# Rotary embedding on one core: the first two slabs in halves through the engines, and the last slab stored in two halves

## Chip, cores and metric

The kernel runs on one core of a Trainium2 chip. The time is device time in microseconds (us), the median over several executions. Kernels that are compared ran on the same chip in the same rounds. A ratio is the mean time of one kernel's fast runs over the mean of the other's fast runs of the same rounds, so it isn't quite the ratio of the medians that are quoted beside it. A difference counts as faster or slower from 2%.

## The reference

```python
batch, seq, dim, num_heads = 16, 512, 1024, 16      # x: float32
x = x.reshape(batch, seq, num_heads, head_dim)       # head_dim 64
x1, x2 = x[..., :32], x[..., 32:]
rotated = np.concatenate([x1 * cos - x2 * sin,
                          x1 * sin + x2 * cos], axis=-1).astype(np.float32)
```

The input and the output are 33.55 MB each, and there are a few operations per element. The cosine and sine tables are 64 KB each.

## The kernel before

The data goes through in 8 slabs of two batches, each [128 x 8192] float32, 4 MB. There are five buffers ("slots"). SyncE issues the loads, ACT issues the stores, so loads and stores have a DMA queue each. Per slab, ACT casts float32 to bfloat16, DVE makes two multiplications and an addition, and ACT casts the result back into the slab, from where it is stored. Load s+5 can only be issued when store s has landed.

```python
    nb = 2; slots = 5
    ...
    load(0)
    ... # the two tables, issued from GpSimd
    for s in range(1, slots):          # loads 1 to 4 wait for the first table
        tc.add_manual_dep(load(s).ins, table[0].ins.name, ...)
    ...
    passes = []
    for s in range(nslabs):
        n = rpp if s < nslabs - 2 else rpp // 2      # the last two slabs in halves
        passes += [(s, r, n) for r in range(0, rpp, n)]

    cast(passes[0])
    for i, (s, r, n) in enumerate(passes):
        if i + 1 < len(passes):
            cast(passes[i + 1])
        ...
        for t, a in ((t2, rpp * hd), (xu, 0)):
            nc.vector.tensor_mul(out=t, in0=xu, in1=view(tab, ...))
        nc.vector.tensor_add(out=xu, in0=xu, in1=view(t2, ...))
        nc.scalar.copy(out=xs, in_=xu)
        if r + n == rpp:
            nc.scalar.dma_start(out=dram(out_flat, s), in_=slab[s])
            if s + slots < nslabs:
                load(s + slots)
```

Of the kernel before, what the change touches and what calls it, by code (L numbers as in the profile page):

```python
# [2 lines left out]

# [4 lines left out]


@with_exitstack  # L10
def kernel(
    ctx: ExitStack,
    tc: tile.TileContext,
    x: bass.AP,
    cos: bass.AP,
    sin: bass.AP,
    num_heads: int,
    out: bass.AP,
):
    nc = tc.nc  # L20
    P = nc.NUM_PARTITIONS

    batch, seq, dim = x.shape
    nh = num_heads
    hd = dim // nh
    half = hd // 2
    bf16 = mybir.dt.bfloat16
    f32 = mybir.dt.float32

    nb = 2  # L30
    slots = 5
    nslabs = batch // nb
    rpp = nb * seq // P
    W = rpp * dim
    SP = seq // rpp
    TW = rpp * half

    out_flat = out.rearrange("b s h d -> b s (h d)")

    singles = ctx.enter_context(tc.tile_pool(name="singles", bufs=1))  # L40
    slabs = ctx.enter_context(tc.tile_pool(name="slabs", bufs=slots))
    xpool = ctx.enter_context(tc.tile_pool(name="xpool", bufs=2))
    psum = ctx.enter_context(tc.tile_pool(
        name="psum", bufs=1, space=bass.MemoryType.PSUM))


    def dram(t, s, a=0, n=W):
        return bass.AP(tensor=t.tensor, offset=t.offset + s * nb * seq * dim + a,
                       ap=[[W, P], [1, n]])


    def view(t, offset, *dims):
        return dataclasses.replace(t, offset=t.offset + offset,
                                   ap=[t.ap[0], *[list(d) for d in dims]])


    slab = {}


    def load(s):  # L60
        slab[s] = slabs.tile([P, W], f32, tag="slab", name="slab")
        return nc.sync.dma_start(out=slab[s], in_=dram(x, s))  # L62


    load(0)


    TR = seq // P
    G = rpp // TR
    table = {}  # L70
    raw = singles.tile([P, 2 * TR * half], f32, tag="raw")
    for i, src in enumerate((cos, sin)):
        table[i] = nc.gpsimd.dma_start(out=view(raw, i * TR * half, (1, TR * half)), in_=bass.AP(  # L73
            tensor=src.tensor, offset=src.offset,
            ap=[[TR * half, P], [1, TR * half]]))



    for s in range(1, slots):
        tc.add_manual_dep(  # L80
            load(s).ins, table[0].ins.name,
            mybir.DependencyInfo(mybir.DependencyClass.Sync,
                                 mybir.DependencyReason.DATA),
            reason="issue")


    pick = singles.tile([P, G * P], bf16, tag="pick")
    nc.gpsimd.memset(pick, 0.0)  # L88
    for g in range(G):
        part = view(pick, g * P, (SP, P // SP), (1, SP))  # L90
        nc.gpsimd.affine_select(  # L91
            out=part, in_=part, compare_op=mybir.AluOpType.not_equal, fill=1.0,
            base=-g, pattern=[[0, P // SP], [-G, SP]], channel_multiplier=1)

    tab1 = singles.tile([P, 2 * TR * half], bf16, tag="tab1")
    nc.vector.tensor_copy(out=tab1, in_=raw)  # L96
    acc = psum.tile([P, 2 * TW], f32, tag="acc")
    for i in range(2):
        for g in range(G):
            nc.tensor.matmul(view(acc, i * TW + g * TR * half, (1, TR * half)),  # L100
                             view(pick, g * P, (1, P)),
                             view(tab1, i * TR * half, (1, TR * half)),
                             start=True, stop=True)

    tab = singles.tile([P, 2 * rpp * hd], bf16, tag="tab")
    nc.vector.tensor_copy(out=view(tab, 0, (hd, 2 * rpp), (1, half)),  # L106
                          in_=view(acc, 0, (half, 2 * rpp), (1, half)))
    nc.vector.tensor_copy(out=view(tab, half, (hd, rpp), (1, half)),  # L108
                          in_=view(acc, 0, (half, rpp), (1, half)))
    nc.vector.tensor_scalar_mul(  # L110
        out=view(tab, rpp * hd + half, (hd, rpp), (1, half)),
        in0=view(acc, TW, (half, rpp), (1, half)), scalar1=-1.0)

    xb = {}


    def cast(u):
        s, r, n = u
        if r == 0:
            xb[s] = xpool.tile([P, W], bf16, tag="xb", name="xb")  # L120
        nc.scalar.copy(out=view(xb[s], r * dim, (1, n * dim)),  # L121
                       in_=view(slab[s], r * dim, (1, n * dim)))



    passes = []
    for s in range(nslabs):
        n = rpp if s < nslabs - 2 else rpp // 2
        passes += [(s, r, n) for r in range(0, rpp, n)]


# [4 lines that stand above are left out]
        xs = view(slab[s], r * dim, (1, n * dim))  # L136
        xu = view(xb[s], r * dim, (1, n * dim))

        t2 = view(slab[s].bitcast(bf16), 2 * r * dim, (1, n * dim))
        for t, a in ((t2, rpp * hd), (xu, 0)):  # L140
            nc.vector.tensor_mul(  # L141
                out=t, in0=xu,
                in1=view(tab, a + r * hd, (hd, n), (0, nh), (1, hd)))
        nc.vector.tensor_add(  # L144
            out=xu, in0=xu, in1=view(t2, half, (hd, n * nh), (-half, 2), (1, half)))

        nc.scalar.copy(out=xs, in_=xu)  # L147
        if r + n == rpp:
            nc.scalar.dma_start(out=dram(out_flat, s), in_=slab[s])  # L149
            if s + slots < nslabs:  # L150
                load(s + slots)


# [1 line left out]
_INS = ['x', 'cos', 'sin', 'num_heads']  # L155
_OUTS = [((16, 512, 16, 64), 'float32')]

_NUMBERS = {'num_heads': 16}


# [26 lines left out]
```

## Time and profile before

| what | before |
|---|---|
| time, median (range) | 162.97 us (162.37 to 163.03, 3 runs) |
| span of the profiled run | 160.1 us |
| DVE, ACT busy | 108.7 us, 113.5 us |
| DMA: loads + stores + tables, share of 16 engines | 98.1% |
| moved | 67.24 MB |

The profiled execution of the kernel before took 161.85 us, a little less than the three timed ones.

The prediction below shows most of the lines. Two more are needed here. The first is the summary of the chain of work that ended last, from the page of the kernel before. The second is the first store in its timeline (start in us, duration in us, engine's queue, line).

```profile
DMA 43%; ACT 34%; DVE 13%; issue 1%; ACTq 0%; SPq 0%
```
```profile
41.06 0.38 ACTq L149 DMA_DIRECT2D out_dram<-slab  x1
```

### The profile page before, as it was taken

The numbers are of one execution on the slowest core, as the hardware profiler recorded it, in microseconds if no ns is written. First come the engines' busy times: TensorE is split into PE (matmuls) and PEld (weight loads), VectorE is DVE, ScalarE is ACT, GpSimd is POOL, SyncE is SP. The second block draws the span as 40 slices with busy tenths as digits, with TensorE's granted clock in tenths as the row PEclk, the third lists the DMA queues.
The fourth block names the chain that finished last, engine by engine and source line by source line (L and its number), as shares of the span: only waits on it lengthen the run. The fifth ranks groups of instructions, "written<-read, shape, count | busy, mean of one in ns | idle before, by whom it ended". The sixth has DMA issues, their size and how long they took to land.

```text
span 160.1 us, 153 instructions
## 1 busy us (share of the span) xinstructions
PE 0.6 (0%) x4; PEld 0.4 (0%) x4; DVE 108.7 (68%) x34; ACT 113.5 (71%) x21; POOL 2.3 (1%) x9
## 2 busy tenths in 40 slices
PE   0010000000000000000000000000000000000000
PEld 0000000000000000000000000000000000000000
DVE  0003089999978997999799659976919779970000
ACT  3006939559899899989993999159998699826000
POOL 5000000000000000000000000000000000000000
DMA  6999999999999999999999999999999999999994
GB/s 221 442 418 393 459 459 393 434 475 401 409 377 475 442 393 434 483 393 401 508 401 393 499 418 393 467 450 393 426 483 401 401 508 401 393 499 418 393 467 188
DMA packets 2368, 67.24 MB, mean 420 GB/s; under 512 B 288, under 2 KB 288, under 8 KB 320
## 3 DMA queue, kind: packets, MB, share of 16 engines
q1 hardware_dynamic: 1152, 33.55, 49.3%
q10 hardware_dynamic: 1152, 33.55, 48.6%
q0 software_dynamic: 64, 0.13, 0.2%
HBM read 33.69 MB, written 33.55 MB: 420 GB/s over the span
## 4 chain that ended last, share of the span: by engine, by line
DMA 43%; ACT 34%; DVE 13%; issue 1%; ACTq 0%; SPq 0%
DMA slab<-in_x_dram 25%; ACT slab L147 18%; DMA out_dram<-slab 17%; ACT xb L121 16%; DVE slab L141 4%; DVE xb L141 4%; DVE xb L144 4%; ACTq L149 0%; ACTq L147 0%; SPq L62 0%
## 5 line engine op out<-in xcount | busy, mean ns | idle before, releaser
L121 ACT CAST xb<-slab 128x8192 bf16<-128x8192 f32 (+1 forms) x10 | 56.5, 5652 | 25.2 <-DMA slab<-in_x_dram 24.0
L147 ACT CAST slab<-xb 128x8192 f32<-128x8192 bf16 (+1 forms) x10 | 56.5, 5650 | 7.2 <-DVE xb L144 7.2
L141 DVE TENSOR_TENSOR slab<-xb,tab 128x8192 bf16<-128x8192 bf16 (+1 forms) x10 | 35.7, 3572 | 21.7 <-ACT xb L121 21.6
L141 DVE TENSOR_TENSOR xb<-xb,tab 128x8192 bf16<-128x8192 bf16 (+1 forms) x10 | 35.7, 3572 | 0.3
L144 DVE TENSOR_TENSOR xb<-xb,slab 128x8192 bf16<-128x8192 bf16 (+1 forms) x10 | 35.7, 3572 | 0.3
L96 DVE CAST tab<-raw 128x256 bf16<-128x256 f32 x1 | 0.3, 294 | 11.2 <-DMA raw<-in_sin_dram 11.2
L121 ACT ACT_TABLE_LOAD x1 | 1.3, 1283 | 0.7 <-PEq L168 0.7
L106 DVE CAST tab<-acc 128x512 bf16<-128x512 f32 x1 | 0.7, 692 | 0.7 <-PE acc L100 0.7
L73 POOL DMA_DIRECT2D raw<-in_cos_dram x1 | 0.7, 674 | 0.8 <-POOLq L168 0.8
L100 PE MATMUL acc<-tab,pick 128*128 128x128 bf16 x4 | 0.6, 300 | 11.5 <-DVE tab L96 11.5
L91 POOL TENSOR_SCALAR_AFFINE_SELECT pick<-pick 128x128 bf16<-128x128 bf16 x2 | 0.5, 288 | 0.1
L73 POOL DMA_DIRECT2D raw<-in_sin_dram x1 | 0.5, 534 | 0.0
L100 PEld LDWEIGHTS <-pick 128*128 128x128 bf16 x4 | 0.4, 126 | 11.4 <-issue 8.2
L110 DVE TENSOR_SCALAR tab<-acc 128x256 bf16<-128x256 f32 x1 | 0.4, 416 | 0.0
L108 DVE CAST tab<-acc 128x256 bf16<-128x256 f32 x1 | 0.4, 415 | 0.0
L88 POOL MEMSET pick<- 128x256 bf16 x1 | 0.3, 330 | 0.0
L168 POOL MEMSET const-float32-0.0<- 128x1 f32 x1 | 0.1, 98 | 0.2 <-issue 0.2
L168 POOL MEMSET const-bfloat16-1.0<- 128x1 bf16 x1 | 0.1, 101 | 0.0
L168 POOL MEMSET const-uint8-127<- 128x1 uint8 x1 | 0.1, 101 | 0.0
L168 POOL MEMSET const-float32-1.0<- 128x1 f32 x1 | 0.1, 99 | 0.0
## 6 DMA issues: line engine op xcount, KB each, us to landing
slab<-in_x_dram SPq DMA_DIRECT2D x8, 4096.0 KB, 26.1
out_dram<-slab ACTq DMA_DIRECT2D x8, 4096.0 KB, 22.9
raw<-in_cos_dram POOLq DMA_DIRECT2D x1, 64.0 KB, 7.2
raw<-in_sin_dram POOLq DMA_DIRECT2D x1, 64.0 KB, 9.2
```

What stands on the lines that cost most here:

```text
L73: table[i] = nc.gpsimd.dma_start(out=view(raw, i * TR * half, (1, TR * half)), in_=bass.AP(tensor=src.tensor, offset=src.offset, ap=[[TR * ...
L88: nc.gpsimd.memset(pick, 0.0)
L91: nc.gpsimd.affine_select(out=part, in_=part, compare_op=mybir.AluOpType.not_equal, fill=1.0, base=-g, pattern=[[0, P // SP], [-G, SP]], c ...
L100: nc.tensor.matmul(view(acc, i * TW + g * TR * half, (1, TR * half)), view(pick, g * P, (1, P)), view(tab1, i * TR * half, (1, TR * half)) ...
L106: nc.vector.tensor_copy(out=view(tab, 0, (hd, 2 * rpp), (1, half)), in_=view(acc, 0, (half, 2 * rpp), (1, half)))
L108: nc.vector.tensor_copy(out=view(tab, half, (hd, rpp), (1, half)), in_=view(acc, 0, (half, rpp), (1, half)))
L110: nc.vector.tensor_scalar_mul(out=view(tab, rpp * hd + half, (hd, rpp), (1, half)), in0=view(acc, TW, (half, rpp), (1, half)), scalar1=-1.0)
L121: nc.scalar.copy(out=view(xb[s], r * dim, (1, n * dim)), in_=view(slab[s], r * dim, (1, n * dim)))
L141: nc.vector.tensor_mul(out=t, in0=xu, in1=view(tab, a + r * hd, (hd, n), (0, nh), (1, hd)))
L144: nc.vector.tensor_add(out=xu, in0=xu, in1=view(t2, half, (hd, n * nh), (-half, 2), (1, half)))
L147: nc.scalar.copy(out=xs, in_=xu)
L168: nc = _bacc.Bacc("TRN2", target_bir_lowering=False, num_devices=1)
```

## The change

The intent is to fill and drain the pipeline faster. In halves, slabs 0 and 1 reach their store sooner. The first half of the last slab can be stored while its second half is still computed, so that only half a store is left after the last write-back. The manual dependency keeps the order of issue and is no semaphore wait.

```diff
-        n = rpp if s < nslabs - 2 else rpp // 2
+        n = rpp if 2 <= s < nslabs - 2 else rpp // 2
@@
-        nc.scalar.copy(out=xs, in_=xu)
-        if r + n == rpp:
+        back = nc.scalar.copy(out=xs, in_=xu)
+        if s == nslabs - 1:
+
+            if r > 0:
+                tc.add_manual_dep(
+                    back.ins, part.ins.name,
+                    mybir.DependencyInfo(mybir.DependencyClass.NoSync,
+                                         mybir.DependencyReason.DATA),
+                    reason="issue")
+            part = nc.scalar.dma_start(
+                out=dram(out_flat, s, r * dim, n * dim), in_=xs)
+        elif r + n == rpp:
             nc.scalar.dma_start(out=dram(out_flat, s), in_=slab[s])
```

## The prediction

> **What bounds the kernel now.** I read the page's engine totals and its DMA queues first, then the waits of the sync queue, then the timeline of the issues. The engine totals and the slices:
>
> ```profile
> PE 0.6 (0%) x4; PEld 0.4 (0%) x4; DVE 108.7 (68%) x34; ACT 113.5 (71%) x21; POOL 2.3 (1%) x9
> ...
> DMA  6999999999999999999999999999999999999994
> ...
> q1 hardware_dynamic: 1152, 33.55, 49.3%
> q10 hardware_dynamic: 1152, 33.55, 48.6%
> q0 software_dynamic: 64, 0.13, 0.2%
> ```
>
> No compute engine is above 71%, but the DMA row is full from the second slice to the last but one. The loads (q1), the stores (q10) and the tables (q0) take 49.3 + 48.6 + 0.2 = 98.1% of 16 engines' span, which is 157.1 of 160.1 us. Only 3.0 us are without a packet. The trace says where those are: the first packet starts at 1.74 us and the last one ends near 158.9, which makes 1.7 + 1.2 = 2.9 us. So there is next to no hole between the first and the last packet. One store takes 0.486 x 160.1 / 8 = 9.7 us of all 16 engines.
>
> The landings agree. The first load has landed at 13.50 us, the last store at 159.20. Between them lie 15 more slab transfers (7 loads, 8 stores): 145.7 / 15 = 9.71 us each, the same while only loads run (13.50, 23.22, 32.94, 42.65), while both directions run, and while only stores run. The mix does not change the rate.
>
> The end of the chain, from the timeline and from the DMA issues of two short windows (the store of slab 6, then that of slab 7; the last number is the time from issue to landing):
>
> ```profile
> 132.50 0.34 ACTq L149 DMA_DIRECT2D out_dram<-slab  x1
> ...
> 146.68 0.34 ACTq L149 DMA_DIRECT2D out_dram<-slab  x1
> ```
> ```profile
> out_dram<-slab ACTq DMA_DIRECT2D x1, 4096.0 KB, 17.0
> ```
> ```profile
> out_dram<-slab ACTq DMA_DIRECT2D x1, 4096.0 KB, 12.5
> ```
>
> The seventh store lands at 132.5 + 17.0 = 149.5 us, the eighth at 146.7 + 12.5 = 159.2. They are 9.7 us apart, one full-rate transfer, so the last store stood behind the one before it for 149.5 - 146.7 = 2.8 us. The **data is ready before the DMA engines are**, even at the very end. The chain of waits names ACT for 34% and DVE for 13%, but it is followed through last releasers and does not show that the queue in front of each store was still full.
>
> **What the Trainium skill says.** "DMA: Bandwidth & Descriptors", Specifications, gives a fabric ceiling of 435 GB/s for the 16 engines. The trace agrees: 4,194,304 bytes in 9.71 us is 432 GB/s, so this kernel is at the ceiling. The same page, Queues, rings and completion order, says that each engine takes turns between its queue rows packet by packet. The trace agrees in the sum: load 4 and store 0 share the engines from about 42.65 and are both in at 62.22 us, two transfers in 19.6 us. "Perfetto Trace Analysis", DMA Optimizations, says that splitting DMAs may let some start sooner if the DMA engines are generally idle; here they are 98% busy, so its condition is not met. "VectorE: DVE Perf Modes", The TRN2 errata, says VectorE and ScalarE pay a fixed cost per instruction. The groups by form agree:
>
> ```profile
> L121 ACT CAST xb<-slab 128x8192 bf16<-128x8192 f32 x6 | 42.1, 7018 | 18.0 <-DMA slab<-in_x_dram 16.7 <-ACT slab L147 1.3
> ...
> L144 DVE TENSOR_TENSOR xb<-xb,slab 128x8192 bf16<-128x8192 bf16 x6 | 26.6, 4425 | 0.2
> ...
> L121 ACT CAST xb<-slab 128x4096 bf16<-128x4096 f32 x4 | 14.4, 3603 | 7.3 <-DMA slab<-in_x_dram 7.3
> ...
> L144 DVE TENSOR_TENSOR xb<-xb,slab 128x4096 bf16<-128x4096 bf16 x4 | 9.2, 2292 | 0.1
> ```
>
> A cast cut in two costs 2 x 3.603 - 7.018 = 0.19 us more, a tensor operation 2 x 2.292 - 4.425 = 0.16 us more.
>
> **The change, part by part.**
>
> Slabs 0 and 1 in halves. This adds 4 casts on ACT (4 x 0.19 = 0.75 us) and 6 operations on DVE (6 x 0.16 = 0.96 us). Both engines wait for loads at that time, so none of it is on the path. What it moves: the first half-cast runs 13.5 to 17.1; DVE works on both halves in the order of the changed program (two multiplies of the first half, one of the second, then its add) and is done with six operations of 2.32 us, pauses included, at 17.1 + 13.9 = 31.0; ACT casts half of slab 1 at 23.2 to 26.8, then writes slab 0 back in halves, the second at 31.0 to 34.6. Store 0 is thus issued at about **34.7 us instead of 41.06**, 6.4 us sooner. Store 1, worked out in the same way, comes at 52.5 instead of 55.45. Store 2 comes at 69.2 instead of 69.80, and there the lead is gone, because ACT and DVE alternate with slab-long steps from then on.
>
> What is that worth? Count transfers. By time t the engines have moved 1 + (t - 13.50) / 9.71 slabs. At 41.06 that is 3.84, while five loads had been issued: 1.16 slabs, or 11 us of work, were still queued. The same sum at each later issue before gives 6.6 us at store 1, between 9 and 20 us at those that follow, 7.2 at store 6 and 2.8 at store 7. It is never zero. Bringing a store forward by 6 us into a queue that already holds 11 us of work changes the order in which the packets go, not when the last one goes. **Worth: 0.0 us.** Loads 3 and 4 now share the engines with store 0 and land later (I estimate 49 and 68 us instead of 42.65 and 59.79), and loads 5 to 7 end within about 3 us of before. I carried this ledger, with even sharing, to the end: stores 6 and 7 would be ready around 134 and 148 us, about 1 us later than before.
>
> The last slab stored in halves. It adds one DMA issue (0.34 us of ACT's sequencer) and turns 128 packets of 32 KiB into 256 of 16 KiB. The trace has packets of 32 KiB at 1.213 us and of 4 KiB (the tables) at 0.159, which is 0.008 us fixed plus 27.2 bytes per ns; eight more packets on each engine are 8 x 0.008 = 0.07 us. What it moves: the first half can be issued after its own write-back, about 141 us, the second about 148. Store 6 keeps the engines busy until 149.5, so the first half stands in line for some 8 us and the second for about 6. **Worth: between 0.0 and 0.1 us lost**, plus the insurance that a last store ready 1 us later than before has no hole in front of it.
>
> The head (1.7 us, and the tables' packets before 13.50) and the tail (0.9 us from the last landing to the end) are untouched. Sum: 162.97 + 0.07, and I round down a little since one of the three runs before was at 162.37: 162.9 us.
>
> **The rivals.** First, the gain that the chain of waits promises: half a store less at the end (9.7 / 2 = 4.9 us) and a pipeline that starts 6.4 us sooner, which would make 158 to 160 us. For it speaks only the chain, and ACT's 24 us of waiting for loads; against it the 2.8 us for which the last store already queued, and the 98%. It needs a hole in the DMA row, and there is none. Second, a new wait: the early stores take engine time from loads 3 and 4, the casts from slab 4 on come later, and the last stores are issued so late that the queue runs dry before them. A delay of 1 us in the middle is covered by the leads; to show, the last slab's first half would have to come over 8 us later. It would make 163.5 to 165 us. Third, costs per packet and per issue of the split store are larger than the tables' packets suggest, or the two directions together cost HBM something at a different overlap: 163.2 to 164. Against it stands that 9.71 us holds in each mix before.
>
> **Range and chances.** With the DMA as bound, the answer is the time before within its scatter; the runs before spread over 0.66 us, and kernels on the same chip agree to about 0.3%, or 0.5 us. I widen that slightly on both sides for the second and third rivals and for a small gain: 162.2 to 163.7. Over 2% is 3.3 us. A gain of that size would need more than all of the 3.0 us without packets; a loss needs a hole that the ledger doesn't show. So 0.02 faster, 0.96 same, 0.02 slower.
>
> **What the profile after would show.** Right, if: the shares of q1 and q10 still add up to about 98% and the DMA row has no slice below 9 inside; store 0 is issued near 34.7 and its landing comes many us after; the last two landings are about 4.9 us apart and the last is at 159 to 159.5; ACT's busy time rises by about 0.75 and DVE's by about 0.96 us; loads 3 and 4 land later than before. Wrong, if the last landing is before 158, which would mean that the engines moved more than 432 GB/s or started sooner, or if a slice of the DMA row is thin, which would mean that a load or the split store arrived at an empty queue.

## The result and the profile after

The changed kernel takes 162.84 us (162.58 to 163.17, 6 runs) against 162.95 us (162.37 to 163.09, 6 runs): ratio 1.0001, 95% interval 0.998 to 1.0023. Nothing moved. The profiled execution was the slowest of the six, 163.17 us, with a span of 161.0 us. That of the kernel before was faster than all its timed runs here (161.85 us), so the 0.9 us between the two spans compare a fast execution with a slow one; the medians of six are 0.1 us apart, the other way round.

From the page of the changed kernel, the busy times, the DMA row of the 40 slices, the three DMA queues and the summary of the chain:

```profile
PE 0.6 (0%) x4; PEld 0.4 (0%) x4; DVE 109.3 (68%) x40; ACT 113.8 (71%) x25; POOL 2.3 (1%) x9
...
DMA  7999999999999999999999999999999999999994
...
q1 hardware_dynamic: 1152, 33.55, 49.3%
q10 hardware_dynamic: 1296, 33.56, 48.3%
q0 software_dynamic: 64, 0.13, 0.2%
...
DMA 43%; ACT 23%; DVE 21%; issue 3%; SPq 0%; ACTq 0%
```

The DMA queues take 97.8% of a span 0.9 us longer, 157.5 against 157.1 us, and the DMA row has no thin slice inside. Meanwhile the chain has changed a lot: ACT from 34% to 23%, DVE from 13% to 21%. A view that shifts by ten points while the time stays put doesn't show the bound of this kernel.

The timeline after has the first store and the two pieces of the last one at these times:

```profile
34.41 0.38 ACTq L159 DMA_DIRECT2D out_dram<-slab  x1
...
139.52 0.34 ACTq L156 DMA_DIRECT2D out_dram<-slab  x1
...
146.53 0.34 ACTq L156 DMA_DIRECT2D out_dram<-slab  x1
```

The first store is issued 6.65 us sooner. The next four fences are DMA issues of short windows, one issue each. The last number is the time from issue to landing. First store 0 before, then store 0 after:

```profile
out_dram<-slab ACTq DMA_DIRECT2D x1, 4096.0 KB, 21.2
```
```profile
out_dram<-slab ACTq DMA_DIRECT2D x1, 4096.0 KB, 24.9
```

It lands at 41.06 + 21.2 = 62.3 before and at 34.41 + 24.9 = 59.3 after. Of the 6.65 us, 3.7 go at once into a longer transfer, because the loads are still in the way. By the same trace the loads pay for the rest: load 3 lands at 47.80 instead of 42.65, load 4 at 67.16 instead of 59.79. Then the two pieces of the last store, after:

```profile
out_dram<-slab ACTq DMA_DIRECT2D x1, 2048.0 KB, 15.5
```
```profile
out_dram<-slab ACTq DMA_DIRECT2D x1, 2048.0 KB, 13.4
```

They land at 139.52 + 15.5 = 155.0 and at 146.53 + 13.4 = 159.9. A 2 MB piece at full rate takes 4.9 us. Both pieces spent most of their time in line. The first piece was ready 7 us sooner than a whole store would have been, and that was all in the queue.

To see idle time that the tenths hide, I added up from the packet records of the trace the time with no data packet (the idle time of the 16 engines, added up and divided by 16):

| stretch, us | before | after |
|---|---|---|
| 0 to 10 | 2.0 | 2.0 |
| 10 to 150 | 0.0 | 0.0 |
| 150 to the last packet | 0.3 | 0.7 |

### The profile page after: what moved, and what is told of

Read it like the earlier page. It is cut to its first block, busy times and chain, and to the rows that moved or that the text cites. A ratio compares the mean times of both kernels' runs of the same rounds, so it can differ in the third digit from the quotient of the medians.

```text
span 161.0 us, 165 instructions
## 1 busy us (share of the span) xinstructions
PE 0.6 (0%) x4; PEld 0.4 (0%) x4; DVE 109.3 (68%) x40; ACT 113.8 (71%) x25; POOL 2.3 (1%) x9
## 4 chain that ended last, share of the span: by engine, by line
DMA 43%; ACT 23%; DVE 21%; issue 3%; SPq 0%; ACTq 0%
DMA slab<-in_x_dram 25%; DMA out_dram<-slab 18%; ACT slab L147 13%; ACT xb L121 10%; DVE xb L144 7%; DVE xb L141 7%; DVE slab L141 7%; SPq L62 0%; ACTq L147 0%
## 5 line engine op out<-in xcount | busy, mean ns | idle before, releaser
L121 ACT CAST xb<-slab 128x4096 bf16<-128x4096 f32 (+1 forms) x12 | 56.8, 4740 | 25.6 <-DMA slab<-in_x_dram 24.8
L147 ACT CAST slab<-xb 128x4096 f32<-128x4096 bf16 (+1 forms) x12 | 56.9, 4740 | 6.3 <-DVE xb L144 6.3
L141 DVE TENSOR_TENSOR slab<-xb,tab 128x4096 bf16<-128x4096 bf16 (+1 forms) x12 | 36.0, 3001 | 21.0 <-ACT xb L121 20.9
L144 DVE TENSOR_TENSOR xb<-xb,slab 128x4096 bf16<-128x4096 bf16 (+1 forms) x12 | 36.0, 3002 | 0.4
L141 DVE TENSOR_TENSOR xb<-xb,tab 128x4096 bf16<-128x4096 bf16 (+1 forms) x12 | 36.0, 3002 | 0.4
L96 DVE CAST tab<-raw 128x256 bf16<-128x256 f32 x1 | 0.3, 293 | 11.1 <-DMA raw<-in_sin_dram 11.1
```

The costliest lines, as they stand in the source:

```text
L121: nc.scalar.copy(out=view(xb[s], r * dim, (1, n * dim)), in_=view(slab[s], r * dim, (1, n * dim)))
L141: nc.vector.tensor_mul(out=t, in0=xu, in1=view(tab, a + r * hd, (hd, n), (0, nh), (1, hd)))
L144: nc.vector.tensor_add(out=xu, in0=xu, in1=view(t2, half, (hd, n * nh), (-half, 2), (1, half)))
L147: back = nc.scalar.copy(out=xs, in_=xu)
```

## The experiments

Theory: from 10 us on the DMA engines always have a packet, so work that is made ready sooner only queues longer. An earlier store is worth the empty engine time in front of it, which is zero here. First rival: one part gains and the other gives it back. Second rival: the compute chain is the bound after all, and something in the chain ate the gain.

| run | time, us (median) | before in the same rounds | ratio (95% interval) |
|---|---|---|---|
| first_only | 162.66 | 162.49 | 1.0014 (0.9988 to 1.004) |
| last_only | 163.24 | 162.49 | 1.0045 (1.0013 to 1.0078) |
| before_late2 | 164.81 | 162.49 | 1.0125 (1.0073 to 1.0178) |
| after_late2 | 162.68 | 162.49 | 1.001 (0.9977 to 1.0042) |
| before_half (wrong result) | 142.89 | 162.28 | 0.8803 |
| after_half (wrong result) | 146.47 | 162.28 | 0.9019 |
| before_mid (wrong result) | 149.35 | 162.42 | 0.9192 |
| after_mid (wrong result) | 146.38 | 162.42 | 0.9014 |
| before_slots3 | 198.88 | 162.28 | 1.2247 |
| after_slots3 | 188.63 | 162.28 | 1.1629 |
| head_free | 163.05 | 162.31 | 1.0024 (0.9983 to 1.0065) |
| head_act | 164.76 | 162.31 | 1.0126 (1.0087 to 1.0164) |

### Each part alone

first_only takes the kernel before with `n = rpp if 2 <= s < nslabs - 2 else rpp // 2`. last_only takes the changed kernel with the old line:

```diff
-        n = rpp if 2 <= s < nslabs - 2 else rpp // 2
+        n = rpp if s < nslabs - 2 else rpp // 2
```

> Only the first part of the change: slabs 0 and 1 in halves, the last slab stored whole. Theory (the DMA engines have work queued at every moment, so a store brought forward only changes the order of packets): ratio to before 0.997 to 1.003, store 0 issued near 34.4 us, the last landing near 159.2 to 159.9. Rival (the early stores gain time at the front and the split store gives it back at the end, or the other way round): this kernel alone differs from before by at least 1%, with the other part alone moving the opposite way.

> Only the second part: the last slab stored in two halves, slabs 0 and 1 whole. Theory: ratio 0.997 to 1.003; the first half is issued near 139.6 and stands behind store 6 until about 149, the two last landings are 4.9 us apart. Rival (the chain of waits names the true bound, so half a store is saved at the end): ratio about 0.97, or a movement opposite to that of the first part alone.

Neither part moves the time by 1%, and neither moves it down, so there is no gain in one part that the other gives back. In first_only, store 0 is issued at 34.23 and the last landing is at 159.60. In last_only the pieces are issued at 138.61 and 145.62, and the last two landings are 154.63 and 159.47. The ratio of last_only, 1.0045, lies just above what I expected, and its interval excludes 1. Both parts together, with the same split store, gave 1.0001. I can't say what these 0.7 us are. The extra packets should cost 0.07 us by the packet durations. It stays open, and it is far below 2%.

### Using up the lead

The lead is the time that a finished store still stands in line behind the packets of others. To use it up, DVE repeats a multiplication twice before the last half slab. It writes the values that are written anyway, so the result stays right.

```diff
+        if s == nslabs - 1 and r > 0:
+            for _ in range(2):
+                nc.vector.tensor_mul(
+                    out=t2, in0=xu,
+                    in1=view(tab, rpp * hd + r * hd, (hd, n), (0, nh), (1, hd)))
         for t, a in ((t2, rpp * hd), (xu, 0)):
```

> The kernel before, with two more VectorE operations of 2.3 us each (a repeated multiply that writes the same values, result right) ahead of the last half slab, so that the last store is issued 4.6 us later, near 151.3 us. Theory: the lead of 2.8 us is used up; the DMA engines run dry when store 6 is done, and the end moves by about 151.3 + 1.0 (issue to first packet on idle engines, as for the first load) - 148.9 (where the last store's packets began before) = 3.4 us, to some 166.4 us, ratio 1.02. If the compute chain were the bound, the whole 4.6 us would show (167.6). If leads were far larger than I read, nothing would show.

> The changed kernel with the same two extra operations: the second half of the last store is issued near 151.1 instead of 146.5 us. Theory: the first half of that store keeps the engines busy until about 154, so the delay is hidden: 162.6 to 163.3 us, ratio 0.997 to 1.005, and 3 us less than the kernel before with the same delay. If the compute chain were the bound here, it would take 4.6 us more, 167.5.

The same 4.6 us of extra compute cost the kernel before 2.3 us in the medians, and the changed kernel nothing (0.2 us, within the interval). The table by stretches of the two profiles shows why. The columns are the stretch, its length, the busy us of PE, PEld, DVE, ACT and POOL, the clock, the busy share of the DMA engines and their GB/s. First the kernel before with the delay, then the changed kernel with it:

```profile
148.00:152.00 4.00, 0.00 (x0) 0.00 (x0) 0.28 (x1) 3.60 (x1) 0.00 (x0) 1.00 0.02 8
```
```profile
148.00:152.00 4.00, 0.00 (x0) 0.00 (x0) 0.00 (x0) 3.27 (x1) 0.00 (x0) 1.00 0.84 360
```

In the first, 8 GB/s: store 6 had given its last packets and the last store, issued at 152.0, was not there yet. That hole is 3.8 us of engine time in the packet records, the span of that profile is 164.0 us, and the other profile, 161.0, has no such hole because the first piece of the split store fills it. The 2.3 us are less than the 3.4 expected. Two of the four runs took 165.6 and 165.7 us and two 163.9 and 164.0, that is 3.2 and 1.4 us above the median before, and the profiled run was one of the slow pair. The expected loss fits the slow pair alone. What sets the pair of a run wasn't tried. By the 2% rule the loss of 1.25% counts as no difference, but its interval excludes 1.

This is the clearest test of the bound: compute that is in time is free, compute that comes later than the queue's lead costs. It also gives the size of the lead. The last store of the kernel before with the delay, issued into idle engines, and its time from issue to landing:

```profile
152.00 0.34 ACTq L154 DMA_DIRECT2D out_dram<-slab  x1
```
```profile
out_dram<-slab ACTq DMA_DIRECT2D x1, 4096.0 KB, 11.1
```

So a whole store takes 11.1 us where nothing stands in front of it, 1.4 us more than its 9.7 us of packets. Of the 12.5 us without the delay, only 1.4 were queue. The two profiles agree: the last store was issued 5.3 us later (152.00 against 146.68) and landed 3.9 us later (163.1 against 159.2). (Of the 5.3 us, 0.7 are no added compute: load 7 landed that much later in this profile.) A 2 MB store on idle engines takes 6.3 us (the last store of before_mid below), so the last piece of the changed kernel, with 13.4, had 7.1 us in reserve. That is what the split store is worth and the plain time doesn't show.

### Making the DMA engines faster than the compute

If the theory holds, the change must help once the DMA engines have time to spare. Each store writes only half of each partition's bytes.

```diff
-            nc.scalar.dma_start(out=dram(out_flat, s), in_=slab[s])
+            nc.scalar.dma_start(out=dram(out_flat, s, 0, W // 2),
+                                in_=view(slab[s], 0, (1, W // 2)))
```

In the changed kernel each piece of the last slab is halved in the same way.

> The kernel before, but each store writes only the first half of each partition's 32 KiB (result wrong on purpose: the rest of the output is not written). DMA work falls by 8 x 4.86 = 39 us, to about 13.5 + 7 x 9.71 + 8 x 4.86 = 120 us, below the 113.5 us of ACT plus its 13.5 us of waiting at the start. Theory: the DMA engines stop being the bound, ACT with its 14.35 us per slab takes over, 143 to 152 us.

> The changed kernel with the same halved stores (the last slab in two stores of a quarter slab). Theory: once the DMA engines aren't the bound, both parts of the change show: the steady stores come about 1.0 us sooner (store 2 at 68.8 instead of 69.8 in the full kernels) and the last transfer is 2.4 instead of 4.9 us long, so 2.5 to 4.5 us less than the kernel before with halved stores. If the change were worth nothing by itself (its extra instructions eat its gain), the two halved kernels would be within 1 us of each other.

The order came out the other way round: the changed kernel is 3.6 us slower. The timelines show that my experiment was at fault. First the last store issue of the kernel before with half stores, then that of the changed one:

```profile
133.16 0.34 ACTq L149 DMA_DIRECT2D out_dram<-slab  x1
```
```profile
139.46 0.34 ACTq L156 DMA_DIRECT2D out_dram<-slab  x1
```

The half of each partition that I stored is exactly the half that the first write-back of a split slab produces. So the kernel before stored its last slab after the first write-back, and only the changed one waited for the second. The time of before_half itself, 142.89 us, came out just below the 143 to 152 that I had expected. The pair was mended by storing the middle half, which needs both write-backs:

```diff
-            nc.scalar.dma_start(out=dram(out_flat, s), in_=slab[s])
+            nc.scalar.dma_start(out=dram(out_flat, s, W // 4, W // 2),
+                                in_=view(slab[s], W // 4, (1, W // 2)))
```

> Mends the earlier pair with halved stores. There the stored half of each partition was exactly the half that the first write-back of a split slab makes, so the kernel before could issue its last store after the first half's write-back (133.2 us) while the changed kernel waited for the second (139.5): the pair compared the wrong thing. Here each store writes the middle half of each partition's 32 KiB, which needs both write-backs (result wrong on purpose). Theory: the last store of the kernel before is issued near 140.3 us, and lands as long after its issue as in the earlier run: 149 to 151 us. If the earlier pair's order was not due to that dependency, this kernel stays near 143.

> The changed kernel with the middle half of each stored piece. Nothing about its dependencies changes against the earlier halved run of it, so 146 to 147.5 us again. Theory: 2.5 to 4.5 us less than the kernel before with the middle half stored: about 0.8 us from the earlier write-backs and 2.5 us from a last transfer of a quarter instead of half a slab. If the two are within 1 us of each other, the change is worth nothing even where the DMA engines have spare time.

The DMA row of before_mid shows that the engines do have time to spare, in the last quarter of the span:

```profile
DMA  6999999999997999999999989998905800660085
```

Now the changed kernel is 3.0 us faster, 146.38 against 149.35, some 2%; no run of one lies within 2.6 us of a run of the other. The last issue of before_mid and its time from issue to landing, then the last issue of after_mid:

```profile
140.38 0.34 ACTq L149 DMA_DIRECT2D out_dram<-slab  x1
```
```profile
out_dram<-slab ACTq DMA_DIRECT2D x1, 2048.0 KB, 6.3
```
```profile
139.18 0.34 ACTq L156 DMA_DIRECT2D out_dram<-slab  x1
```

The last write-back ends 1.2 us sooner, and the last transfer is 2.4 us shorter from issue to landing (143.06 - 139.18 = 3.88 against 146.66 - 140.38 = 6.28). That makes 3.6 us by the traces; the two profiled spans differ by 3.3. So the change does what it was meant to do, and with full stores there is no place for it to show.

### Opening holes in the DMA queue

With 3 buffers, fewer loads can be queued ahead, and the engines stand idle before the first store.

```diff
-    slots = 5
+    slots = 3
```

> The kernel before with 3 slab buffers instead of 5. Only three loads can be queued ahead; they are in at 32.9 us, and store 0 is issued at 41.1, so the DMA engines stand idle from about 33 to 42. Theory: this hole of 9 us isn't made up, and later holes come where a load can be issued only when a store has landed: 172 to 185 us.

> The changed kernel with 3 slab buffers. Store 0 is issued at 34.4, so the first hole is about 2.5 instead of 9 us. Theory (an early store is worth exactly the empty time of the DMA engines in front of it): 3 to 7 us less than the kernel before with 3 buffers. If early stores were worthless or harmful by themselves, because they slow the loads, the two would be equal or this one slower.

With 3 buffers the change is worth 10.25 us, 188.63 against 198.88, or 5%. The stretch between the last queued load and the first store, in the kernel before with 3 buffers and then in the changed one (the last two columns are the DMA share and GB/s):

```profile
34.00:42.00 8.00, 0.00 (x0) 0.00 (x0) 7.97 (x2) 7.56 (x2) 0.00 (x0) 1.00 0.13 57
```
```profile
34.00:42.00 8.00, 0.00 (x0) 0.00 (x0) 7.55 (x4) 8.00 (x4) 0.00 (x0) 1.00 0.92 393
```

Both sizes were off. The packet records say that this first hole is 9.8 us before and 3.3 after, so 6.5 us come from the halves of the first slabs. Another 4.3 us come from the end: there is a hole of 4.4 us before the last whole store and of 0.1 before the second piece of the split one. I had left the second part of the change out of the expectation. 6.5 + 4.3 = 10.8 us of empty time. The agreement with the measured 10.25 us is rough: the packets of the changed kernel took 1.4 us more in all (164.4 against 162.9 us), and the two profiled spans differ by 9.1. The level is higher than expected (198.9 instead of 172 to 185) since I had underrated the other holes: about 2 us at each of the five loads that wait for a store, and 6.4 us before the seventh store. In all, 32.8 us without a data packet before and 22.1 after. Some 6 us of the level are no holes: the packets of the kernel before took 162.9 us with 3 buffers and 157.0 with 5. Why wasn't tried.

### Is there anything to win at the head?

The changed kernel with loads 1 to 4 issued at once (head_free), and with the two tables on ACT's queue besides (head_act):

```diff
     for s in range(1, slots):
-        tc.add_manual_dep(load(s).ins, table[0].ins.name, ...)
+        load(s)
```
```diff
-        table[i] = nc.gpsimd.dma_start(out=view(raw, ...), in_=...)
+        table[i] = nc.scalar.dma_start(out=view(raw, ...), in_=...)
```

> The changed kernel, with loads 1 to 4 issued at once instead of after the first table has landed. Before, load 0 has its packets spread from 1.75 to 13.8 us, though 8 packets of 1.213 us on each engine are 9.7 us: some 1 to 2 us of the engines' time are lost there. Theory (only empty DMA time can be won): these are won, the time falls by 0.8 to 2 us, to 161 to 162.2. Rival: the tables then land so late behind the loads' packets that the first multiply, and all after it, is late; with leads of over 6 us that costs nothing unless the tables come after about 20 us.

> As the run before, and the two tables are issued from ACT's queue at the very start instead of from GpSimd's. Theory: tables land before the first load, the engines have no gap from 1.8 us on: 160.8 to 162.2 us, the same as or up to 0.5 us below the run before.

Both expectations fell. In head_free load 0 still occupies the engines from 1.75 us until the packets of load 1 begin at 12.47 (12.44 in the kernel before), so the engines were not empty there. Of load 0's 128 packets, 15 took longer in head_free, up to 2.2 us instead of 1.21, and 16 in the kernel before; queueing more loads doesn't help. (The 13.8 us in the expectation is too late: load 0 had landed at 13.50.)

head_act is slower by 1.3%, under 2% but with an interval that excludes 1, and 1.7 us slower than head_free in the same rounds. From its page, the DMA packets and the issues of the tables (the last number is us from issue to landing):

```profile
DMA packets 2736, 67.24 MB, mean 413 GB/s; under 512 B 304, under 2 KB 560, under 8 KB 560
...
raw<-in_cos_dram ACTq DMA_DIRECT2D x1, 64.0 KB, 12.8
raw<-in_sin_dram ACTq DMA_DIRECT2D x1, 64.0 KB, 22.3
```

And the same from the page of head_free, which differs in nothing but that GpSimd issues them:

```profile
DMA packets 2512, 67.24 MB, mean 417 GB/s; under 512 B 304, under 2 KB 304, under 8 KB 336
...
raw<-in_cos_dram POOLq DMA_DIRECT2D x1, 64.0 KB, 7.4
raw<-in_sin_dram POOLq DMA_DIRECT2D x1, 64.0 KB, 9.3
```

From GpSimd the two tables go in 32 packets of 4 KiB, from ACT in 256 of 512 bytes, 16 on each engine. The sine table is in at 1.16 + 22.3 = 23.5 us instead of 11.3. That fits engines that give each queue one packet in turn: the second table's eight small packets per engine then wait for eight loads' packets of 1.21 us, 9.7 us, and it lands 9.9 us after the first. The multiplications begin at 25.96 instead of 17.34 us, and store 0 comes at 43.23 instead of 34.62. Yet the engines have no hole of that size. Their packets just add up to 159.1 us instead of 157.4. Why they take longer in all is open; most of the excess is where the two queues first compete, between 40 and 90 us.

None of the runs with a right result beats both kernels.

## Why the prediction was right

**The bound.** That the DMA engines, not the chain, set the end is shown from three sides: no hole between 10 and 150 us in either kernel, a delay of compute that is free until it exceeds the lead, and a gain that appears as soon as the engines have time to spare.

**The early stores.** Store 0 was expected near 34.7 us and came at 34.41; store 1 at 52.5 and came at 51.85; store 2 at 69.2 and came at 68.78. Loads 3 and 4 were expected at 49 and 68 and landed at 47.80 and 67.16. "Worth: 0.0" agrees with first_only.

**The end.** Stores 6 and 7 were expected about 1 us later than before, near 134 and 148. They came at 132.41 and 146.53, slightly sooner than before, so the ledger was 1.5 us too late there; which of its steps, wasn't traced. The two pieces landed 4.85 us apart (155.03 and 159.88), as expected. The last landing was expected by 159.5 and was 159.88: the 16 engines of the last store finished between 159.04 and 159.88, in the kernel before between 158.68 and 159.20.

**The lead.** The prediction has the last store stand in line for 2.8 us, from the issue of one store to the landing of another. It thereby counts as queue what a store takes to start and to be reported as landed. The lead was 1.4 us, by before_late2. The conclusion holds, but with half the margin, and the ledger's leads at the other stores, worked out in the same way, are presumably too large as well.

**A citation that the sum doesn't test.** Two transfers in 19.6 us come out whichever way the engines take turns. The packet counts do show equal turns: between 50 and 55 us the kernel before moved 32 packets of each queue. And the page on splitting ties idle engines to the whole task ending sooner, not to a part starting sooner. With the busy engines neither happened: the first piece was issued 7 us sooner, but its first packet came at 149.0 us, and that of the whole store before near 148.6.

**A term of the wrong size.** ACT's busy time was to rise by 0.75 us and DVE's by 0.96. They rose by 0.3 and 0.6. The halves do last 3.602 and 2.291 us each, as these groups of the changed kernel show (count, then total busy us and mean ns):

```profile
L121 ACT CAST xb<-slab 128x4096 bf16<-128x4096 f32 x8 | 28.7, 3602 | 21.3 <-DMA slab<-in_x_dram 21.3
...
L144 DVE TENSOR_TENSOR xb<-xb,slab 128x4096 bf16<-128x4096 bf16 x8 | 18.3, 2291 | 0.2
```

But two instructions that follow each other overlap: two half casts that start at 13.50 together take 7.11 us in the timeline, not 7.20. So a cut costs 0.09 us there, half of the 0.19 that I had worked out from the durations. None of it was on the path.

**The rivals.** The first rival, the gain of 3 to 5 us that the chain promises, is refuted for this kernel, and after_mid shows the state in which it would be right. The second, loads so late that the last stores meet an empty queue, did not happen: store 6 and both pieces of the last store came on time. Of the third, costs of the split store, last_only leaves 0.45% (interval 0.13 to 0.78%), not explained.

## What to carry to other kernels

Before shortening a path that ends in a transfer, add up the DMA queues' shares and ask how much is queued in front of that transfer when it is issued; time from issue to landing, minus what the same transfer takes from issue to landing on idle engines, is the time that it spent behind and between the packets of others. (Minus the time of its packets alone, it comes out 1.4 us too long here.) As long as it isn't zero, making the data ready sooner was worth nothing in this kernel, however much of the chain of waits the engines fill. The same change was worth 2 to 5% where the queue ran empty, and it can be kept as a reserve against lateness.

## What the Trainium skill lacked or had wrong

- "DMA: Bandwidth & Descriptors", Issuing engine by pattern, calls DMAs issued from the sync and scalar queues generally faster than those from GpSimd. For the two 64 KB tables beside full loads the reverse was measured: 12.8 and 22.3 us from ACT's queue in 512-byte packets, 7.4 and 9.3 us from GpSimd's in 4 KiB packets. It is one exception to a general statement; transfers of other sizes weren't tried.
- The same page, Latency and other measured facts, gives about 0.6 us to the first byte for those queues. On idle engines the runs agree, counted from the end of the issuing instruction: the first packet came 0.6 us after it for load 0 and 0.5 us for the delayed last store (0.85 to 1.0 us from its start). With the engines full, the first packet of store 0 came 3.4 to 4.6 us after the start of its issue (41.02 to 44.47 in last_only, 41.06 to 45.62 in the kernel before). The page has no figure for the second state.
